# The last 512 features of an output projection computed with tokens as rows, and the last two recurrent heads' products spaced differently

## The chip, the cores and the metric

The kernel runs on one core of a Trainium2 chip. The metric is the device time of one execution in microseconds (us). The kernel before takes 1165.85 us, the median of three runs (1165.79 to 1166.35). A core has a matrix engine (TensorE, PE in the profile; PEld is its weight load), a vector engine (VectorE, DVE), an engine for activations and copies (ScalarE, ACT), a general one (GpSimd, POOL) and a queue engine for transfers (SyncE, SP). Each engine works through its own list of instructions in order and waits on semaphores for the others.

## The reference

One step of a two-layer decoder: layer 0 is a gated linear recurrence (HGRN2, 16 heads of 128), layer 1 is attention with a sliding window and sinks. Both end in an output projection and a LayerNorm over the residual. What matters here is that end, which layer 1 runs last of all, and the gated output of the recurrence:

```python
ALPHA = (2.0 * DEPTH) ** 0.25

# layer 0: o is the recurrence's output for 16 heads, g a projection of x
o = o * rsqrt(mean(o ** 2) + RMS_EPS) * norm_w            # per head
y = (o.reshape(bsz, t, 2048) * silu(g)) @ w_out           # 2048 x 2048

# layer 1: o is the attention's output
y = (o * silu(g)) @ w_out                                 # 2048 x 2048

# both
x = ALPHA * x + y
x = (x - mean(x)) * rsqrt(var(x) + LN_EPS) * ln_g + ln_b  # over 2048 features
```

There are 256 prompt tokens (and 16 meta tokens in layer 0, which are dropped after it) and 64 sample tokens, 8 sequences of 8. Everything is float32, and the LayerNorm of layer 1 gives the outputs `y_prompt` (256 x 2048) and `y_sample` (64 x 2048).

## The kernel before, in words

All activations lie with features as rows (partitions) and tokens as columns: `xh[k]`, `xl[k]` are feature block k (of 16) of the hidden state, split into a rounded high part and the remainder. A projection tile is 128 output features by all tokens. It is a sum over 16 feature blocks of three matmuls each, weight-low times x-high, weight-high times x-low, weight-high times x-high (lines 210 to 212). The weights (`lo`, `hi`) are what TensorE loads, 128x128, and the tokens are the moving columns: 336 in layer 0, 320 in layer 1's end.

The class `Stream` sets the order. It runs a list of chunks, each four feature blocks of one tile. After every feature block it calls `step()`, which advances up to two of the waiting "side" generators by one piece; a generator's `yield n` says after how many steps it wants its next turn. All work that isn't a projection (heads, epilogues, residuals) is interleaved with the projections in this way, and the written order is the order on each engine. The weights come ahead: `raw` (line 144) loads 512 KB pieces on SP's queue, 14 chunks ahead, into four buffers; `conv_hi` (L155, ACT) and `conv` (L166, DVE) make the two parts, some four to seven chunks ahead, in ten buffers.

**End of the recurrence.** Each head has a tail: `psp` and `pss` (state products, L657 and L661), `po` (its output, L689 to L701), the sum of squares and its power (`ss`, L706 to L708), `osc` (scaling, DVE L711), three transposes of osc (L717, into the bank `lv_b` of the next head, or `pt` for the last), and the gated output (L722) split into `oh`, `ol`. The projection tiles `z` of layer 0 read those. For the last head a fixed list of waits in steps says when head 14's and head 15's tails advance between the first z tiles. The first three z tiles, z0 to z2, are run chunk by chunk in turn. Their accumulators are three banks (`pj`) used before by the last tiles of the input projection, of which head 15's gate g is the last: DVE's L440 (`sg`, times g) is its reader.

**End of layer 1.** Sixteen tiles y0 to y15 of 128 features. For each, `residuals()` makes the LayerNormed hidden state `res` (POOL L1237, DVE L1239, POOL L1241, ACT L1243); `epi_y` adds it (DVE L1276, L1278), transposes the result to tokens as rows (L1286, three blocks: two of prompt tokens, one that holds the 64 sample tokens twice), takes the statistics (L1290) and multiplies by `ln_g` (L1302, L1306) into `z` and `zs`. After the last tile `stats()` (L1341 to L1368) finishes mean and power, makes a small matrix SL by a transpose, and `final_norm()` (L1371 to L1404) adds the mean and `ln_b` terms: nine matmuls R of SL with rows of g and b, then DVE (L1396) or ACT and POOL (L1392, L1393), and the twelve output transfers. `gb_parts()` prepares the rows of g and b beside the tiles, and `open_y()` loads g broadcast to all partitions on SP's queue.

## Time and profile before

| | |
|---|---|
| median of three runs | 1165.85 us |
| the profiled execution | 1166.44 us, its span 1164.2 us |
| mean granted clock of TensorE | 0.993 |
| TensorE busy | 1144.6 us, 98% of the span |
| VectorE busy | 789.5 us, 68% |
| ScalarE busy | 613.3 us, 53% |
| GpSimd busy | 237.9 us, 20% |
| transfers | 171.67 MB, 147 GB/s in the mean |
| z tiles of layer 0 | first product 570.3 us, last 701.0 us |
| y tiles of layer 1 | first product 1030.2 us, last 1147.6 us |

The span goes from the first to the last instruction of the profiled execution; some two microseconds lie around it. Overlapping matmuls are shown with their own length, so a matmul of "0.32 us" may start 0.15 us after the one before it. A row of the trace's timeline has the start, the duration, the engine, the line of the kernel, the operation, output and inputs, shapes, the count, and in brackets how long the engine had been idle and what released it.

### The profile page before, as it was taken

The page shows a single profiled execution, that of the slowest core. Times are in us where ns is not written, and L with a number is a line of the kernel's source. Part 1 is how long each engine was busy: PE and PEld are TensorE (multiplying, and loading weights), DVE is VectorE, ACT ScalarE, POOL GpSimd, SP SyncE. Part 2 cuts the span into 40 slices and gives each one's busy share as a digit, 9 for nine tenths or more (in the row PEclk, how much of TensorE's full clock was granted, in tenths as well). Part 3 has the DMA queues.
Part 4 walks back from the last instruction along what each step waited for, and adds up shares of the span by engine and source line. Part 5 has one row for each costly group of instructions (what it writes and reads, how often), then busy time and mean ns, then how long its engine had stood idle before and what let it go on. Part 6 is the DMA issues. An engine that isn't in the chain of part 4 may idle for free.

```text
span 1164.2 us, 26517 instructions
## 1 busy us (share of the span) xinstructions
PE 1144.6 (98%) x10225; PEld 1111.5 (95%) x10225; DVE 789.5 (68%) x2130; ACT 613.3 (53%) x1730; POOL 237.9 (20%) x344
## 2 busy tenths in 40 slices
PE   9999999999999999999899999999999999999995
PEld 8999999999999999999899999998999999999994
DVE  4766666666566666576668776577877767777674
ACT  5664555544555545554545444566666555554431
POOL 2131221211221212211224332100000112144311
PEclk9999999999999999999999999999999999999997
DMA  9644565454565455555445555643443535556532
GB/s 254 196 137 133 163 181 148 137 154 136 163 183 144 135 147 150 165 169 142 133 133 141 146 145 160 202 129 105 127 115 105 137 110 163 145 151 188 144 95 90
DMA packets 328908, 171.67 MB, mean 147 GB/s; under 512 B 19164, under 2 KB 325532, under 8 KB 328742
## 3 DMA queue, kind: packets, MB, share of 16 engines
q1 hardware_dynamic: 327184, 167.77, 51.6%
q8 instruction: 80, 1.31, 0.5%
q0 software_dynamic: 640, 1.18, 0.3%
q10 hardware_dynamic: 960, 1.05, 0.3%
q14 instruction: 44, 0.36, 0.1%
HBM read 157.17 MB, written 14.42 MB: 147 GB/s over the span
## 4 chain that ended last, share of the span: by engine, by line
PE 95%; DVE 1%; ACT 1%; DMA 1%; POOL 0%; issue 0%; SPq 0%; POOLq 0%; DVEq 0%
PE pj_g L210 7%; PE pj_g L211 7%; PE pj_g L212 7%; PE pj_q L210 7%; PE pj_q L211 6%; PE pj_q L212 6%; PE pj_f L210 3%; PE pj_z L212 3%; PE pj_z L211 3%; PE pj_z L210 3%; PE pj_i L210 3%; PE pj_f L211 3%; PE pj_i L212 3%; PE pj_i L211 3%; PE pj_f L212 3%; PE pj_y L210 3%
## 5 line engine op out<-in xcount | busy, mean ns | idle before, releaser
L210 PE MATMUL pj_q<-xh,wlo_q 128*128 128x336 f32 (+1 forms) x512 | 163.2, 319 | 0.0
L210 PE MATMUL pj_g<-xh,wlo_g 128*128 128x336 f32 (+1 forms) x512 | 163.0, 318 | 0.0
L211 PE MATMUL pj_g<-xl,whi_g 128*128 128x336 f32 (+1 forms) x512 | 160.7, 314 | 0.0
L211 PE MATMUL pj_q<-xl,whi_q 128*128 128x336 f32 (+1 forms) x512 | 160.6, 314 | 0.0
L212 PE MATMUL pj_g<-xh,whi_g 128*128 128x336 f32 (+1 forms) x512 | 160.5, 313 | 0.0
L212 PE MATMUL pj_q<-xh,whi_q 128*128 128x336 f32 (+1 forms) x512 | 160.3, 313 | 0.0
L210 PEld LDWEIGHTS pj_q<-xh,wlo_q 128*128 128x128 f32 x512 | 96.6, 189 | 2.5 <-issue 1.4
L210 PEld LDWEIGHTS pj_g<-xh,wlo_g 128*128 128x128 f32 x512 | 96.6, 189 | 0.7 <-issue 0.3
L211 PEld LDWEIGHTS pj_g<-xl,whi_g 128*128 128x128 f32 x512 | 96.8, 189 | 0.0
L211 PEld LDWEIGHTS pj_q<-xl,whi_q 128*128 128x128 f32 x512 | 96.7, 189 | 0.0
L212 PEld LDWEIGHTS pj_g<-xh,whi_g 128*128 128x128 f32 x512 | 96.6, 189 | 0.0
L212 PEld LDWEIGHTS pj_q<-xh,whi_q 128*128 128x128 f32 x512 | 96.6, 189 | 0.0
L166 DVE TENSOR_TENSOR wlo_g<-raw_g,whi_g 128x512 fp32r<-128x512 f32 x128 | 91.0, 745 | 0.2 <-ACT whi_g L155 0.2
L155 ACT CAST whi_g<-raw_g 128x512 fp32r<-128x512 f32 x128 | 76.5, 623 | 22.2 <-DMA raw_g<-in_hgrn_w_in_dram 17.7
L166 DVE TENSOR_TENSOR wlo_q<-raw_q,whi_q 128x512 fp32r<-128x512 f32 x128 | 85.1, 684 | 2.8 <-ACT whi_q L155 2.8
L619 POOL TENSOR_TENSOR vm<-Vs,cst 96x512 fp32r<-96x512 f32 x32 | 33.7, 1054 | 252.5 <-DVE Vs L616 251.5
L210 PE MATMUL pj_f<-xh,wlo_f 128*128 128x336 f32 x256 | 82.6, 323 | 0.0
L210 PE MATMUL pj_z<-oh,wlo_z 128*128 128x336 f32 x256 | 81.9, 320 | 0.0
L212 PE MATMUL pj_z<-oh,whi_z 128*128 128x336 f32 x256 | 81.6, 319 | 0.0
L210 PE MATMUL pj_i<-xh,wlo_i 128*128 128x336 f32 x256 | 81.5, 318 | 0.0
L211 PE MATMUL pj_z<-ol,whi_z 128*128 128x336 f32 x256 | 81.5, 318 | 0.0
L211 PE MATMUL pj_f<-xl,whi_f 128*128 128x336 f32 x256 | 81.1, 317 | 0.0
(398 smaller groups left out, 3229.1 us busy)
## 6 DMA issues: line engine op xcount, KB each, us to landing
raw_z<-in_hgrn_w_out_dram SPq DMA_DIRECT2D x32, 512.0 KB
raw_q<-in_swa_w_in_dram SPq DMA_DIRECT2D x32, 512.0 KB
raw_g<-in_swa_w_in_dram SPq DMA_DIRECT2D x32, 512.0 KB
raw_y<-in_swa_w_out_dram SPq DMA_DIRECT2D x32, 512.0 KB
raw_f<-in_hgrn_w_in_dram SPq DMA_DIRECT2D x30, 512.0 KB
raw_q<-in_hgrn_w_in_dram SPq DMA_DIRECT2D x30, 512.0 KB
raw_i<-in_hgrn_w_in_dram SPq DMA_DIRECT2D x30, 512.0 KB
raw_g<-in_hgrn_w_in_dram SPq DMA_DIRECT2D x30, 512.0 KB
```

The lines of the kernel that those rows point to most:

```text
L155: e.nc.scalar.copy(hi, t["raw", kc])
L166: e.nc.vector.tensor_tensor(lo, t.pop(("raw", kc)), hi.bitcast(F32), op=ALU.subtract)
L210: nc.tensor.matmul(ps, lo[:, kk, :], xh, start=first, stop=False)
L211: nc.tensor.matmul(ps, hi[:, kk, :], xl, start=False, stop=False)
L212: nc.tensor.matmul(ps, hi[:, kk, :], xh, start=False, stop=last)
L619: nc.gpsimd.tensor_tensor(vm[0:96, 4 * u:4 * u + 4, :], Vs[:, u, :].bitcast(F32).unsqueeze(1).to_broadcast([96, 4, P]), cst[0:96, 0:4].uns ...
```

## The change

**Rows instead of columns.** y0 to y11 stay. The last 512 features become one tile `yr` in which the tokens are what TensorE loads (128x128) and the weights are the moving 512 columns. It goes over three blocks of tokens: prompt tokens 0 to 127 and 128 to 255 with three products per feature block, and a third block of the sample tokens, once their high parts and once their low parts (copied to columns 320 to 384 of `ph`), which needs two products. The weights are loaded in runs of 512 columns, 2 feature blocks per transfer, converted per feature block, and all sixteen pairs are kept for blocks 1 and 2; six of the pairs lie in a new pool in the space of the hidden state, which is released before.

**Normalization by block.** The result has tokens as rows already. `normal` takes statistics, power and the LayerNorm of a prompt block and sends it while the next block's products run. `normal_sample` does the sample block after the last product. `stats`, `final_norm` and `gb_parts` go. g and b are loaded broadcast (3 MB in 16 transfers) on POOL's queue.

**Residuals.** Those of the last four feature blocks are made by a second generator beside the other tiles, transposed by 12 transposes `rt` in one go inside tile y6, and copied to `z`, `zs`. The other tiles' transposed results are copied by ACT, without the multiplication by g.

**Heads 14 and 15.** Another list of waits puts head 14's transposes behind more z products.

The core of the diff:

```diff
@@ run
+            if t.get("rows"):
+                while ("hl", kc) not in t:
+                    self.conv(self.nc + 1)
+                t["rows"](t, kc)
+                self.i += 1
+                continue
@@ head_chain, after the last head's products
-            yield 1
-            adv(h - 1)
-            yield 2
-            adv(h - 1)
-            yield 1
-            adv(h - 1)
-            yield 1
-            adv(h - 1)
-            yield 3
-            adv(h)
-            yield 1
-            adv(h)
-            yield 1
-            adv(h)
-            yield 3
-            adv(h)
-            for w in (4, 3, 2, 1):
+            for w, us in ((1, (h - 1,)), (3, (h - 1,)), (6, (h,)), (2, (h - 1, h)), (1, (h - 1, h)), (4, (h,)), (3, (h,)),
+                          (2, (h,)), (4, (h,)), (1, (h,))):
                 yield w
-                adv(h)
+                for u in us:
+                    adv(u)
@@ residuals
+                late = j >= LT
+                r = Y["p1"].tile([P, 384 if late else TY], F32, tag="resl" if late else "res", name=f"res{j}")
...
+                if late:
+                    nc.scalar.activation(r[:, 320:384], r[:, 256:320], AF.Identity, bias=lnb[0][:, j:j + 1])
+                nc.scalar.activation(rr, rr, AF.Identity, bias=lnb[0][:, j:j + 1])
@@ opening
+            for k in range(KT):
+                yield 4
+                nc.scalar.copy(L["oh1"][k][:, 320:384], L["ol1"][k][:, 256:320].bitcast(F32))
...
+            pts = [pm(f"rt{b}") for b in range(3)]
+            for b in range(3):
+                for i in range(4):
+                    nc.tensor.transpose(pts[b][:, 128 * i:128 * i + 128], Y["r", LT + i][:, 128 * b:128 * b + 128],
+                                        ident)
+            yield 1
+            for b in range(2):
+                nc.scalar.copy(Y["z"][:, b, 128 * LT:D], pts[b])
...
+            xps.close()
+            Y["cv"] = yes.enter_context(tc.tile_pool(name="wcx", bufs=6, side="right"))
+            yl = yes.enter_context(tc.tile_pool(name="ygb", bufs=1, side="right"))
+            for nm, src in (("g", ln_g), ("b", ln_b)):
+                t = Y[nm] = yl.tile([P, D], F32, tag=f"y{nm}", name=f"y{nm}")
+                for c in range(4):
+                    cs = slice(512 * c, 512 * c + 512)
+                    nc.gpsimd.dma_start(t[:, cs], src[1:2, cs].to_broadcast([P, 512]))
+                    yield 8
...
@@ epi_y
+                        nc.vector.bn_stats(Y["bn"][:, b, j, :], pt[:, 128 * b:128 * b + 128])
+                    nc.scalar.copy(Y["z"][:, :, 128 * j:128 * j + 128], pt[:, 0:256].rearrange("p (b f) -> p b f", b=2))
...
-                    nc.vector.tensor_tensor(Y["z"][:, :, cs], pt[:, 0:256].rearrange("p (b f) -> p b f", b=2),
-                                            Y["g"][:, cs].unsqueeze(1).to_broadcast([P, 2, P]), op=ALU.mult)
...
+        def block(t, k, b):
+            hi, lo = (x.rearrange("p k c -> p (k c)") for x in t["hl", k])
+            oh, ol = L["oh1"][k], L["ol1"][k]
+            cs = slice(128 * b, 128 * b + 128)
+            pairs = [(oh, lo), (oh, hi)] if b == 2 else [(oh, lo), (ol, hi), (oh, hi)]
+            for i, (x, w) in enumerate(pairs):
+                nc.tensor.matmul(t["ps", b], x[:, cs], w, start=k == 0 and i == 0,
+                                 stop=k == KT - 1 and i == len(pairs) - 1)
+                if i != 1:
+                    st.step()
+
+        def rows(t, k):
...
+            block(t, k, 0)
+            st.conv(st.i + e.DC)
+            if k < KT - 1:
+                return
+            while st.side:
+                st.step()
+            normal(t, 0)
+            for q in range(KT):
+                block(t, q, 1)
+            normal(t, 1)
+            for q in range(KT):
+                block(t, q, 2)
+            normal_sample(t)
...
+        def normal(t, b):
+            z = Y["z"][:, b, 128 * LT:D]
+            nc.vector.scalar_tensor_tensor(z, z, ALPHA, t["ps", b], op0=ALU.mult, op1=ALU.add)
+            nc.vector.bn_stats(Y["ag"][:, b, 3:9], z)
+            rs, nm = moments(b, 9)
...
+            for c, (z, g, bb) in enumerate(part):
+                if c == 0 or not b:
+                    centred(z, g, nm)
+                    if c == 0 and b:
+                        nr = Y["nr"]
+                        nc.vector.tensor_tensor(nr, nm, rs, op=ALU.mult)
+                        for zz, _, _ in part[1:]:
+                            nc.scalar.activation(zz, zz, AF.Identity, bias=nr, scale=rs)
+                    scaled(z, bb, rs)
+                else:
+                    nc.vector.tensor_tensor(z, z, g, op=ALU.mult)
+                    nc.vector.tensor_tensor(z, z, bb, op=ALU.add)
+                nc.sync.dma_start(y_prompt[0, 128 * b:128 * b + 128, 512 * c:512 * c + 512], z)
+
+        def normal_sample(t):
+            zs, S, ag = Y["zs"], t["ps", 2], Y["ag"]
+            for u in range(2):
+                us, fs = slice(64 * u, 64 * u + 64), slice(256 * u, 256 * u + 256)
+                z = zs[us, 768:1024]
+                nc.vector.scalar_tensor_tensor(z, z, ALPHA, S[0:64, fs], op0=ALU.mult, op1=ALU.add)
+                nc.vector.tensor_tensor(z, z, S[64:128, fs], op=ALU.add)
+            nc.vector.bn_stats(ag[:, 2, 3:9], zs[:, 768:1024])
+            nc.scalar.copy(ag[0:64, 2, 9:15], ag[64:128, 2, 3:9])
+            nc.vector.tensor_copy(ag[64:128, 2, 9:15], ag[0:64, 2, 3:9])
+            rs, nm = moments(2, 15)
...
+            for c in range(2):
+                cs = slice(512 * c, 512 * c + 512)
+                centred(zs[:, cs], Y["gs"][:, cs], nm)
+                scaled(zs[:, cs], Y["bs"][:, cs], rs)
...
```

`moments` is the aggregate (DVE), the power (POOL) and the negative mean (DVE); `centred` is (z - mean) x g and `scaled` is z x power + b, one DVE operation each.

What that makes of the engines' lists stands here at three places. A row is the line, the operation, output and inputs with the numbers of their buffers, the shape, and what it waits for. The first place is TensorE at the end of the recurrence, from head 15's transposes (`pv15`) to its `po15`; `pj_z0`, `pj_z1`, `pj_z2` are products of the first z tiles. Before:

```order
L589 MATMUL pv15_8411<-ident_110,iT_149 128x128 x3
L210 MATMUL pj_z0_8364<-oh2_628,wlo_z0_0_8144 128x336
...
L212 MATMUL pj_z1_8465<-oh2_628,whi_z1_0_8136 128x336
L717 MATMUL lv15_b_8371<-ident_110,osc14_8472 128x128 [waits DVE_49,Activation_49]
...
L210 MATMUL pj_z1_8465<-oh3_629,wlo_z1_0_8168 128x336
...
L210 MATMUL pj_z2_8495<-oh0_626,wlo_z2_0_8193 128x336
...
L657 MATMUL psp15_8507<-V15_8428,K15_8429 128x128 [waits PE_49,Activation_49]
...
L661 MATMUL pss15_0_8511<-vm15_8435,Ks15_8433 128x512 [waits PE_49,Pool_49]
...
L210 MATMUL pj_z2_8495<-oh3_629,wlo_z2_0_8193 128x336
...
L212 MATMUL pj_z0_8364<-oh7_633,whi_z0_1_8184 128x336
L689 MATMUL po15_8547<-S15_8518,qi1_161 32x128 [waits DVE_49,Activation_49]
```

Now:

```order
L606 MATMUL pv15_8411<-ident_110,iT_149 128x128 x3
L225 MATMUL pj_z0_8364<-oh2_628,wlo_z0_0_8144 128x336
...
L227 MATMUL pj_z1_8465<-oh3_629,whi_z1_0_8136 128x336
L225 MATMUL pj_z2_8484<-oh0_626,wlo_z2_0_8193 128x336 [waits DVE_49]
...
L227 MATMUL pj_z0_8364<-oh4_630,whi_z0_1_8184 128x336
L660 MATMUL psp15_8506<-V15_8428,K15_8429 128x128 [waits PE_49,Activation_49]
...
L664 MATMUL pss15_0_8510<-vm15_8435,Ks15_8433 128x512 [waits PE_49,Pool_49]
L664 MATMUL pss15_1_8512<-vm15_8435,Ks15_8433 128x512 [waits DVE_49,Activation_49]
L225 MATMUL pj_z0_8364<-oh5_631,wlo_z0_1_8285 128x336
...
L720 MATMUL lv15_b_8371<-ident_110,osc14_8477 128x128 x3
L225 MATMUL pj_z0_8364<-oh7_633,wlo_z0_1_8285 128x336
...
L692 MATMUL po15_8563<-S15_8525,qi1_161 32x128 [waits DVE_49,Activation_49]
```

There were 15 z products ahead of head 14's transposes and 12 between them and `psp15`. Now 33 stand between `pv15` and `psp15`, then the state products, 6 z products, the transposes, and 15 more z products ahead of `po15`. The first product of z2, before the fourth behind the transposes, is the 19th behind `pv15` and has a wait of its own on DVE.

The second place is DVE's list around the last weight pieces. Before, in tiles 13 and 14:

```order
L166 TENSOR_TENSOR wlo_y14_3_15625<-raw_y14_2_15435,whi_y14_3_15587 128x512 [waits Activation_49]
L166 TENSOR_TENSOR wlo_y15_0_15641<-raw_y15_0_15479,whi_y15_0_15612 128x512 [waits DMAHW2_49,Activation_49]
...
L1276 SCALAR_TENSOR_TENSOR z1_13_15674<-res13_15337,pj_y13_15589 128x256 [waits PE_49]
L1278 SCALAR_TENSOR_TENSOR z1_13_15674<-res13_15337,pj_y13_15589 128x128
L166 TENSOR_TENSOR wlo_y15_2_15677<-raw_y15_2_15526,whi_y15_2_15649 128x512 [waits DMAHW3_49,DVE_49,Activation_49]
L1290 BN_STATS ybn_14504<-yt13_15685 128x6 [waits PE_49]
...
L1302 TENSOR_TENSOR yz_14502<-yt13_15685,yg_14506 128x2x128
L1306 TENSOR_TENSOR yzs_14503<-yt13_15685,yg_14506 64x128
L166 TENSOR_TENSOR wlo_y15_3_15700<-raw_y15_2_15526,whi_y15_3_15665 128x512 [waits Activation_49]
L1276 SCALAR_TENSOR_TENSOR z1_14_15739<-res14_15426,pj_y14_15667 128x256 [waits PE_49]
```

Now, from tile 11's end into block 0 of the new tile `yr`:

```order
L170 TENSOR_TENSOR wlo_yr_5_15522<-raw_yr_4_15343,whi_yr_5_15494 128x512 [waits Activation_49]
L1318 SCALAR_TENSOR_TENSOR z1_11_15540<-res11_15218,pj_y11_15446 128x256 [waits PE_49]
L1320 SCALAR_TENSOR_TENSOR z1_11_15540<-res11_15218,pj_y11_15446 128x128
L170 TENSOR_TENSOR wlo_yr_6_15543<-raw_yr_6_15386,whi_yr_6_15514 128x512 [waits DMAHW2_49,DVE_49,Activation_49]
L170 TENSOR_TENSOR wlo_yr_7_15556<-raw_yr_6_15386,whi_yr_7_15530 128x512 [waits Activation_49]
L1331 BN_STATS ybn_14503<-yt11_15552 128x6 [waits PE_49]
...
L1341 BN_AGGR yag_14504<-ybn_14503 128x2 [waits DVE_49] x3
L1342 TENSOR_SCALAR yag_14504<-yag_14504 128x3 [waits DVE_49]
L170 TENSOR_TENSOR wlo_yr_8_15573<-raw_yr_8_15426,whi_yr_8_15547 128x512 [waits DMAHW3_49,Activation_49]
L170 TENSOR_TENSOR wlo_yr_9_15580<-raw_yr_8_15426,whi_yr_9_15558 128x512 [waits Activation_49]
...
L170 TENSOR_TENSOR wlo_yr_15_15622<-raw_yr_14_15545,whi_yr_15_15611 128x512 [waits Activation_49]
L1394 SCALAR_TENSOR_TENSOR yz_14510<-yz_14510,yr0_15532 128x512 [waits PE_49]
```

The pieces `wlo_yr_6` to `wlo_yr_15` stand behind tile 11's additions (`z1_11`), and the last eight of them behind its statistics and aggregations too; all of block 0's products need them in this order.

The third place is DVE's list at the end of the program. Before, from tile 15's last product:

```order
L1276 SCALAR_TENSOR_TENSOR z1_15_15798<-res15_15515,pj_y15_15732 128x256 [waits PE_49]
...
L1290 BN_STATS yag_14505<-yt15_15801 128x6 [waits PE_49]
...
L1344 BN_AGGR mv_15808<-yag_14505 128x2 [waits DVE_49,Pool_49]
...
L1351 TENSOR_SCALAR nm_15814<-mv_15808 128x3 [waits DVE_49]
...
L1358 TENSOR_TENSOR yS_14509<-mM_15815,rstd_15812 128x3x2 [waits DVE_49,Pool_49]
...
L1367 SCALAR_TENSOR_TENSOR yz_14502<-yz_14502,rstd_15812,yb_14511 128x512
L1302 TENSOR_TENSOR yz_14502<-yt15_15801,yg_14506 128x2x128
...
L1396 SCALAR_TENSOR_TENSOR yz_14502<-yz_14502,rstd_15812,R0_15835 128x512 [waits PE_49]
L1396 SCALAR_TENSOR_TENSOR yzs_14503<-yzs_14503,rstd_15812,R2_15839 128x512 [waits PE_49]
L1396 SCALAR_TENSOR_TENSOR yz_14502<-yz_14502,rstd_15812,R3_15841 128x512 [waits PE_49]
L1396 SCALAR_TENSOR_TENSOR yzs_14503<-yzs_14503,rstd_15812,R5_15845 128x512 [waits DVE_49,PE_49]
L1396 SCALAR_TENSOR_TENSOR yz_14502<-yz_14502,rstd_15812,R6_15847 128x512 [waits PE_49]
```

Now, from block 1's normalization (its middle part left out) to the end:

```order
L1394 SCALAR_TENSOR_TENSOR yz_14510<-yz_14510,yr1_15533 128x512 [waits PE_49]
L1395 BN_STATS yag_14504<-yz_14510 128x6 [waits DVE_49]
L1381 BN_AGGR ymv_14505<-yag_14504 128x2 [waits DVE_49]
...
L1405 TENSOR_TENSOR ynr_14508<-ynm_14506,yrs_14507 128x1 [waits Pool_49]
...
L1411 TENSOR_TENSOR yz_14510<-yz_14510,yb_15536 128x512 [waits DVE_49]
L1419 SCALAR_TENSOR_TENSOR yzs_14509<-yzs_14509,yr2_15534 64x256 [waits PE_49]
L1420 TENSOR_TENSOR yzs_14509<-yzs_14509,yr2_15534 64x256 [waits DVE_49]
...
L1421 BN_STATS yag_14504<-yzs_14509 128x6 [waits DVE_49]
L1423 COPY yag_14504<-yag_14504 64x6 [waits DVE_49]
L1381 BN_AGGR ymv_14505<-yag_14504 128x2 [waits DVE_49,Activation_49]
...
L1387 SCALAR_TENSOR_TENSOR yzs_14509<-yzs_14509,ynm_14506,ygs_15450 128x512 [waits DMASW5_49,DMASW3_49,DVE_49]
L1390 SCALAR_TENSOR_TENSOR yzs_14509<-yzs_14509,yrs_14507,ybs_15643 128x512 [waits DMASW3_49,DMASW5_49,DVE_49,Pool_49]
```

The part over all 384 rows that stood behind the last product (statistics, the matrix S, the corrections with R) is gone. What follows the last product (`yr2`) works on the sample rows: four additions of 64x256, statistics, aggregate and two times centred and scaled.

More of the change, by code (lines that the diff above doesn't have):

```diff
@@ L168, in conv, with add_rows @@
             self.nc += 1
+    def add_rows(self, t):
+        self.cseq += [(t, k) for k in range(KT)]
+        self.seq += [(t, k) for k in range(KT)]
     def step(self):
```

214 lines of the change are left out of this document (81 added, 133 removed).

## The prediction

> **What bounds the kernel now.** I read the page's totals first, then the chain that ended last, then TensorE's waits, and last the two places where the change works, instruction by instruction.
>
> ```profile
> span 1164.2 us, 26517 instructions
> PE 1144.6 (98%) x10225; PEld 1111.5 (95%) x10225; DVE 789.5 (68%) x2130; ACT 613.3 (53%) x1730; POOL 237.9 (20%) x344
> PE 95%; DVE 1%; ACT 1%; DMA 1%; POOL 0%; issue 0%; SPq 0%; POOLq 0%; DVEq 0%
> ```
>
> TensorE (PE) is busy for 98% of the span and holds 95% of the chain. So only three things can move the time: the number and length of matmuls, holes in TensorE's stream, and what comes after its last product. TensorE's waits (total, times, longest) name the holes:
>
> ```profile
> PE lv_b L717 <- DVE osc L711: 3.9, 1, 3.9
> PE pS L1363 <- DVE yS L1361: 2.6, 1, 2.6
> ...
> PE ln_rbc L845 <- DVE dg L841: 0.6, 1, 0.6
> ```
>
> The first is head 14's output transposes at the end of the recurrent layer. The second lies in the final normalization, after the last projection product. The change touches both; the third is outside it.
>
> **The junction at 574 to 588 us.** Columns: start, duration, engine, instruction, idle before it.
>
> ```profile
> 573.89 0.49 PE L589 MATMUL pv<-ident,iT 128*128 128x128 f32 x3
> 577.86 0.50 DVE L440 TENSOR_TENSOR sg<-sg,pj_g 128x336 f32<-128x336 f32 x1
> 579.93 0.56 DVE L711 TENSOR_TENSOR osc<-po,ss 128x384 f32<-128x384 f32 x1 [0.96 <-POOL ss L708]
> 580.64 0.88 PE L717 MATMUL lv_b<-ident,osc 128*128 128x128 f32 x3 [3.93 <-DVE osc L711]
> 587.86 0.30 PE L689 MATMUL po<-S,qi 128*32 128x128 f32 x1
> ...
> 563.17 0.94 PE L657 MATMUL psp<-V,K 128*128 128x128 f32 x6
> 564.40 0.49 PE L717 MATMUL lv_b<-ident,osc 128*128 128x128 f32 x3
> ...
> 299.94 0.32 PE L210 MATMUL pj_q<-xh,wlo_q 128*128 128x336 f32 x1
> 305.94 0.32 PE L210 MATMUL pj_q<-xh,wlo_q 128*128 128x336 f32 x1
> ```
>
> The last two rows stand 39 matmuls apart, 6.00 us, so a 336-column product takes 0.1538 us. psp with pss takes 564.40 - 563.17 = 1.23 us. Before, pv ends at 574.38, 15 projection products follow, and then TensorE stands for 3.93 us until head 14's osc is there (579.93 + 0.56). It pays a second time afterwards. Windows of the trace (PE and PEld busy, DVE, ACT, POOL, then the granted clock, DMA share, GB/s):
>
> ```profile
> 580.00:582.00 2.00, 1.36 (x6) 1.39 (x7) 1.53 (x4) 0.00 (x0) 0.80 (x1) 0.61 0.02 7
> 582.00:584.00 2.00, 2.00 (x10) 2.00 (x9) 1.46 (x7) 0.99 (x2) 1.09 (x1) 0.54 0.00 0
> 584.00:586.00 2.00, 2.00 (x16) 1.91 (x15) 0.77 (x3) 0.83 (x3) 0.00 (x0) 1.00 0.00 0
> ...
> 1142.30 0.33 PE yt L1286 x3
> ```
>
> The clock is at half for about 3.4 us. Three transposes take 0.33 us at full clock (last row, from the chain), so what runs from 580.64 to 587.86, 7.22 us, would be 27 x 0.1538 + 1.23 + 0.33 = 5.71 us: 1.51 us more are lost, 5.44 us in all.
>
> Now 33 products stand between pv and psp, then psp and pss, 6 products, the transposes, 15 products and po: 54 instead of 42 before po, twelve of them pulled in front of it. But the 19th of the 33 is the first of tile z2, which waits for DVE: its PSUM bank was pj_g's of head 15, and the sg row frees that only at 578.36. Eighteen products end at 574.38 + 18 x 0.1538 = 577.15, so a new stall of 1.25 us appears (with the 0.04 us between engines, to 578.40). DVE's sg stands behind the Ks and Vs subtractions, which the change does not move. From there 15 products reach 580.71, after osc (580.49), and nothing more waits: 580.71 + 1.23 + 6 x 0.1538 + 0.33 + 15 x 0.1538 = 585.50 for po. Before, po plus the twelve pulled products would be at 587.86 + 12 x 0.1538 = 589.71. **Term 1: -4.2 us.** Its bounds: -5.4 if the new stall does not exist, -2.6 if the stall also costs a clock window. What was hidden by head 14's early transposes is its gated output, which the projection needs only in its last quarter; nothing waits there.
>
> **The last 512 features: products.** For a 320-column product and for a 512-column one (pss, the only such product here):
>
> ```profile
> 1135.54 0.31 PE L210 MATMUL pj_y<-ph,wlo_y 128*128 128x320 f32 x1
> 1141.70 0.31 PE L210 MATMUL pj_y<-ph,wlo_y 128*128 128x320 f32 x1
> ...
> 563.86 0.70 PE L661 MATMUL pss<-vm,Ks 96*128 96x512 f32 x2
> ```
>
> 42 products in 6.16 us are 0.1467 us each. Four tiles of 48, each with three transposes, took 192 x 0.1467 + 4 x 0.33 = 29.49 us. From the end of psp shown above (564.11) to that of pss (564.56) two 512-column products take 0.45 us, 0.225 each; scaling 0.1538 by columns gives 0.2344; from pss's start to the next row's (564.40) it would be 0.27. I take 0.23, between the first two: ends and scaling describe a full stream, as this will be, while a start counts what is filled at its edge. The new 48 + 48 + 32 = 128 products take 29.44 us; tile 11's transposes (0.33) fall among them, and the residuals' 12 transposes, a new burst inside tile 6, cost 4 x 0.33 = 1.31. **Term 2: 29.44 + 0.33 + 1.31 - 29.49 = +1.6 us** (bounds +0.9 at 0.225 and +6.7 at 0.27). So there is no gain on TensorE: the sample block drops one product in three, but the tokens fill 384 rows instead of 320.
>
> **Can block 0 be fed?** These rows group the output stage (busy, mean ns of one):
>
> ```profile
> L166 DVE TENSOR_TENSOR wlo_y<-raw_y,whi_y 128x512 fp32r<-128x512 f32 x64 | 47.4, 772 | 0.2
> L1276 DVE SCALAR_TENSOR_TENSOR z<-res,pj_y 128x256 f32<-128x256 f32 x16 | 6.7, 419 | 23.0 <-PE pj_y L212 23.0
> L1296 DVE BATCH_NORM_AGGREGATE yag<-ybn 128x2 f32<-128x90 f32 x3 | 1.4, 515 | 0.0
> L1290 DVE BATCH_NORM_STATS2 yag<-yt 128x6 f32<-128x128 f32 x3 | 0.7, 288 | 0.4 <-PE yt L1286 0.4
> ...
> 596.38 2.49 DVE L166 TENSOR_TENSOR wlo_z<-raw_z,whi_z 128x512 fp32r<-128x512 f32 x4
> ```
>
> Block 0 eats sixteen weight pieces in 48 x 0.23 = 11.0 us, where the tiles before took a piece per 1.76 us. Six are converted when it starts. DVE owes it ten more at 2.49/4 = 0.62 us back to back, tile 11's two z rows (0.42 and about 0.28 for half the columns), three statistics (0.86) and three aggregations (1.55): 9.3 us, against the 10.35 us at which the last piece is needed. I cost this at nothing; at the mean row's 0.772 it would be 10.8, half a microsecond late (rival 2). Blocks 1 and 2 need no conversions.
>
> **The tail.** The chain after the last product, and the drain:
>
> ```profile
> 1147.76 0.16 PE pj_y L212
> 1150.01 0.90 POOL rstd L1346
> 1152.30 1.69 PE R L1385 x7
> 1157.14 1.22 POOL yz L1393
> ...
> 1158.39 0.34 ACTq L1404 DMA_DIRECT2D out_dram<-yz  x1
> 1161.00:1162.00 1.00, 0.00 (x0) 0.00 (x0) 0.00 (x0) 0.00 (x0) 0.00 (x0) 0.50 1.05 402
> 1162.00:1163.00 1.00, 0.00 (x0) 0.00 (x0) 0.00 (x0) 0.00 (x0) 0.00 (x0) 0.50 0.41 154
> ```
>
> From 1147.92 to 1164.2 are 16.28 us: statistics for 384 rows, the correction's matmuls, POOL's additions, and then twelve output transfers queued behind one another until about 1162.4 (a DMA share of 0.41 in the window from 1162). Now the normalization of blocks 0 and 1 and their transfers run beside blocks 1 and 2, and only 64 tokens remain. Rows for them:
>
> ```profile
> L1396 DVE SCALAR_TENSOR_TENSOR yz<-yz,rstd,R 128x512 f32<-128x512 f32 x4 | 2.9, 744 | 0.4 <-PE R L1385 0.4
> L1344 DVE BATCH_NORM_AGGREGATE mv<-yag 128x2 f32<-128x9 f32 x3 | 0.3, 160 | 0.0
> ```
>
> Block 1 on DVE while block 2 runs (32 x 0.23 = 7.4 us): z 0.74, statistics of 512 values about as much (between 0.288 and four times that), aggregate and nm 0.16 each, centred 0.74, nr 0.16, scaled 0.74, six multiplications and additions at about 0.68 (the conversions' size): 7.5 us, so the sample rows start 0.2 us late at most. They are: four 64x256 operations at 0.42 = 1.68; statistics of 256 values 0.42 (between 0.288 and its double); the exchange of the halves 0.3; aggregate 0.16; POOL's power 0.90, with nm and centred (0.90) beside it; scaled, centred, scaled 2.23; gaps 0.2: 5.9 us. Then four transfers of 128 KB. Old data ended 1.8 us before the span did; issue 0.34, a start of some 0.6 and 256 KB at 300 to 400 GB/s (0.7 to 0.85) make 3.5 us in all (bounds 2.8 without a start, 4.8 if the earlier block's transfers still queue). 0.3 + 5.9 + 3.5 = 9.7 us. **Term 3: 9.7 - 16.28 = -6.6 us** (bounds -7.5 and -5.1).
>
> The Trainium skill, "DMA: Bandwidth & Descriptors", in its fit for a transfer from GpSimd's queue, gives 2.0 us plus the bytes over 436 GB/s. By it the last 256 KB would take an estimated 2.6 us, and the sum would be 0.9 us lower; I stay with the rows of the drain.
>
> The old multiplications by g (32 on DVE) go; 48 small copies on ACT, half idle, replace them beside TensorE, and the late residuals go through POOL, 20% busy. I cost them at nothing: their cover is TensorE's 84 us of tiles 0 to 11, and without it a tile's chain could wait for POOL's residual, up to 1 us once.
>
> **Sum:** -4.2 + 1.6 - 6.6 = -9.2. The profiled execution took 1166.44 us (its span and 2.2 around it), 0.6 above the runs' median of 1165.85, so 1157.2 on its own time and 1156.7 on the median's. I say 1157.0.
>
> **Rivals.** *1. The clock falls after the new stall.* A hole of 1.25 us need not be free:
>
> ```profile
> 712.00:714.00 2.00, 2.00 (x15) 2.00 (x14) 1.52 (x4) 1.28 (x5) 1.78 (x5) 1.00 0.46 131
> 1150.00:1151.00 1.00, 0.00 (x0) 0.00 (x0) 0.97 (x4) 0.00 (x0) 0.89 (x1) 0.73 0.00 0
> ```
>
> For it: in the tail the clock fell in 1150 to 1151 though matmuls ran until 1147.92 and transposes after, so less than 3.4 us of a hole were enough there. Against: at 712 to 714, just behind the 0.6 us hole of ln_rbc, it stayed at 1.00. 1.25 lies between. Price: the 1.5 us measured at the junction, so 1158.5. The Trainium skill, "TensorE: Matmul & The Clock Gate", Part 1, says that the clock drops after at least one idle window of about 3.4 us. By that rule the hole costs no clock and 1157.0 stands; the trace agrees at 580 us and does not clearly in the tail.
>
> *2. Block 0 starves.* DVE at 0.772 per piece is 0.5 us late; the loads too must come at 512 KB per 1.38 us, 380 GB/s, near the 402 that the drain row shows, with four buffers. Late DVE also pushes block 1's normalization past block 2. About +2.5 us: 1159.5. Against: six pieces are ready and the rest of the loads were issued long before.
>
> *3. The other side: the broadcast of g and b holds off the weights.* It is 3 MB on POOL's queue, all issued in tiles 8 to 11 as soon as the space of the hidden state is free.
>
> ```profile
> masks<-in_consts_dram POOLq DMA_DIRECT2D x1, 528.0 KB, 6.7
> 1045.00:1050.00 5.00, 5.00 (x37) 4.99 (x36) 2.23 (x5) 1.18 (x3) 2.52 (x2) 1.00 1.05 329
> ```
>
> If POOL's queue gave what the masks' load shows (528 KB in 6.7 us, 79 GB/s) and the weights nothing meanwhile, the burst would last 40 us; the weights are loaded 14 pieces of 1.76 us ahead, 24 us, so TensorE would stand 16 us: 1173, slower. It decides from a blockade of about 24 + 9 = 33 us. Against it: at 1045 to 1050 the broadcast of g (there on SP) ran at 329 GB/s beside the weights, and TensorE was busy for 5.00 of 5.00 us; weights need 149 GB/s, so at 329 the 3 MB last 17 us beside them. The readers are late in any case: g is first wanted 11 us into the row blocks.
>
> **How the numbers follow.** Forecast 0.64, with its own range 1155.0 to 1159.0 (term 1 without the stall, term 3 at its bounds, term 2 at 0.2344). Rival 1 0.13, rival 2 0.15, rival 3 0.05. The remaining 0.03 is a product cost near 0.27, which gives 1162; with small stalls it is a no-change case. Measurement of this kernel tells 0.2%, 2.3 us, so faster means below 1163.5. Faster 0.91, same 0.04, slower 0.05. The range 1153.9 to 1161.5 takes the forecast and the first two rivals in, up to 2 us of rival 2 beyond its price.
>
> **What would show it.** At the junction: TensorE's wait for osc gone from the list of waits, a wait of 1.2 us of z2's first product for sg in its place, po's start near 585.5, granted clock 1.00 throughout (a window below 1 is rival 1). In the row blocks: products 0.23 us apart, 11 us per prompt block, no wait for wlo (rival 2 would show as one in block 0). In the tail: about 6 us of DVE rows of 64x256 and 128x512 after the last product, 9.7 us to the end, and the clock there without effect since TensorE has nothing left. A TensorE wait for wlo or raw pieces in tiles 8 to 11 is rival 3. The prediction is wrong at its root if TensorE needs 0.27 us per product, or if the wait at the junction only moves to another head's rows.

## The result, and the profile after

The changed kernel takes 1158.84 us (median of four runs, 1157.71 to 1159.38), beside 1166.1 us for the kernel before on the same chip. The ratio is 0.9926 with a 95% interval of 0.9906 to 0.9946. On another occasion the same kernel, run five times more, had a median of 1158.09 us beside 1166.46 (ratio 0.9927, 0.9914 to 0.9939). Forecast were 1157.0 and a range of 1153.9 to 1161.5.

The profiled execution took 1157.71 us with a span of 1155.7; that of before took 1166.44 with 1164.2. The head of its page, and the engines' shares of the chain that ended last:

```profile
span 1155.7 us, 26360 instructions
PE 1141.5 (99%) x10151; PEld 1104.2 (96%) x10151; DVE 795.2 (69%) x2094; ACT 620.2 (54%) x1771; POOL 238.9 (21%) x343
PE 95%; DVE 2%; DMA 1%; ACT 1%; issue 0%; SPq 0%; POOL 0%; DVEq 0%
```

The first rows of TensorE's waits (us in total, times, longest):

```profile
PE pj_z L225 <- DVE sg L457: 1.3, 1, 1.3
PE pw L319 <- DVE mhalf L274: 1.1, 1, 1.1
```

Both large waits of before (3.9 us for osc, 2.6 us for the matrix S) are gone. One of 1.3 us is new: tile z2's first product waits for the last head's gate. The second, at the start of the program, was there before. Here is the junction in the timeline of the change (start, duration, engine, instruction, idle before it and its releaser):

```profile
573.61 0.49 PE L606 MATMUL pv<-ident,iT 128*128 128x128 f32 x3
577.59 0.50 DVE L457 TENSOR_TENSOR sg<-sg,pj_g 128x336 f32<-128x336 f32 x1
578.15 0.42 PE L225 MATMUL pj_z<-oh,wlo_z 128*128 128x336 f32 x1 [1.26 <-DVE sg L457]
585.37 0.30 PE L692 MATMUL po<-S,qi 128*32 128x128 f32 x1
```

And the windows of the change behind it; the third number from the right is the granted clock:

```profile
578.00:580.00 2.00, 1.85 (x12) 1.85 (x13) 0.93 (x3) 1.94 (x6) 1.90 (x2) 1.00 0.86 258
580.00:582.00 2.00, 2.00 (x15) 1.91 (x14) 1.96 (x3) 0.27 (x1) 0.95 (x2) 1.00 0.02 6
```

The hole is 1.26 us, where 1.25 were forecast, and the clock stays at 1.00. From pv to po it takes 585.37 - 573.61 = 11.76 us; the forecast had 585.50 - 573.89 = 11.61. Before, the same way took 13.97 us with twelve products fewer, 15.82 with them: the junction gained 4.06 us.

The end of the program, from the chain of the change that ended last (start, duration, engine, line):

```profile
1115.50 1.38 PE yr L1356 x6
1116.89 0.45 PE yt L1328 x3
1117.34 20.69 PE yr L1356 x90
...
1145.01 0.69 DVE yz L1411
1145.70 0.33 DVE yzs L1419
1147.40 0.44 DVE yag L1421
1150.89 0.75 DVE yzs L1390
```

And its last windows, with DMA share and GB/s at the right:

```profile
1153.00:1154.00 1.00, 0.00 (x0) 0.00 (x0) 0.00 (x0) 0.00 (x0) 0.00 (x0) 0.50 0.91 251
1154.00:1155.00 1.00, 0.00 (x0) 0.00 (x0) 0.00 (x0) 0.00 (x0) 0.00 (x0) 0.50 0.00 1
```

96 products of 512 columns take 22.07 us, 0.230 each, and follow one another without a hole in this execution except for 0.12 us at `yt` (0.45 in place of 0.33). The last 32 bring the last product's end to about 1138.03 + 32 x 0.23 = 1145.39. VectorE is then 0.3 us late with block 1's last part (its end is at 1145.70), works on the sample rows until 1151.64, and the data are out by about 1154; the span ends at 1155.7. So the tail is 10.3 us, of which 4.1 lie behind the last operation: 2.4 until the data are out and 1.7 behind them. Before, the data moved longer than the prediction's windows of one microsecond let it seem. In half a microsecond of the kernel before, less than 1.7 us ahead of the span's end (1164.2):

```profile
1162.50:1163.00 0.50, 0.00 (x0) 0.00 (x0) 0.00 (x0) 0.00 (x0) 0.00 (x0) 0.50 0.15 57
```

### The profile page after: what moved, and what is told of

It is laid out like the page before. It is cut to its first block, busy times and chain, and to the rows that moved or that the text cites. A ratio compares the mean times of both kernels' runs of the same rounds, so it can differ in the third digit from the quotient of the medians.

```text
span 1155.7 us, 26360 instructions
## 1 busy us (share of the span) xinstructions
PE 1141.5 (99%) x10151; PEld 1104.2 (96%) x10151; DVE 795.2 (69%) x2094; ACT 620.2 (54%) x1771; POOL 238.9 (21%) x343
## 3 DMA queue, kind: packets, MB, share of 16 engines
q8 instruction: 80, 1.31, 0.5%
## 4 chain that ended last, share of the span: by engine, by line
PE 95%; DVE 2%; DMA 1%; ACT 1%; issue 0%; SPq 0%; POOL 0%; DVEq 0%
PE pj_g L225 7%; PE pj_g L226 7%; PE pj_g L227 7%; PE pj_q L225 7%; PE pj_q L226 6%; PE pj_q L227 6%; PE pj_f L225 3%; PE pj_i L225 3%; PE pj_z L225 3%; PE pj_f L226 3%; PE pj_i L227 3%; PE pj_z L227 3%; PE pj_i L226 3%; PE pj_f L227 3%; PE pj_z L226 3%; PE pj_y L225 2%
```

## The experiments

All times are medians; each group names the kernel before that ran beside it. TensorE's wait for the very first input varies between executions (0.4 to 1.3 us in the traces here), so places of two traces are compared by distances, not by their clock times.

### The two parts apart

The change without the new spacing, and the spacing alone on the kernel before:

```diff
# rows_only: the change, with the old list for the last head
-            for w, us in ((1, (h - 1,)), (3, (h - 1,)), (6, (h,)), ...):
-                yield w
-                for u in us:
-                    adv(u)
+            yield 1
+            adv(h - 1)
...
# spacing_only: the kernel before, with the new list
-            yield 1
-            adv(h - 1)
...
+            for w, us in ((1, (h - 1,)), (3, (h - 1,)), (6, (h,)), ...):
```

> The change without the new spacing of heads 14 and 15 (their old list of waits). Theory: the parts add up, and the spacing is worth 4.2 us, so this kernel is 4.2 us slower than the change, about 1163.0 us or 3.1 us below the kernel before; TensorE waits 3.9 us for head 14's osc again, with the clock near half behind it. Rival: the gain is all in the row blocks and the tail, and the stall at the junction is made good later by something else that would have waited; then it equals the change, 1158.8.

> The kernel before with only the new list of waits of heads 14 and 15. Theory: 4.2 us faster than the kernel before, about 1161.9, with a stall of 1.26 us of tile z2's first product on the gate's multiplication in place of the 3.9 us. Rival: the freed time is lost again before layer 0 ends (another wait appears in the z tiles): within 1 us of before.

Beside 1166.57 us before, the rows alone took 1163.24 (1161.67 to 1164.49; ratio 0.9975, 0.9965 to 0.9984) and the spacing alone 1161.62 (ratio 0.9961, 0.9949 to 0.9974). So the parts are worth 3.3 and 4.9 us, and their sum, 8.3, is what the change gives (7.3 and 8.4 in its two measurements). The traces show the two patterns in TensorE's waits, first with the rows alone, then with the spacing alone:

```profile
PE lv_b L734 <- DVE osc L728: 3.9, 1, 3.9
```

```profile
PE pS L1349 <- DVE yS L1347: 2.6, 1, 2.6
PE pj_z L210 <- DVE sg L440: 1.3, 1, 1.3
```

The spacing gave what was expected. In its trace po comes 11.75 us behind pv (573.31 to 585.06), 4.07 better than before with the twelve products counted in; pv itself stands 0.6 us earlier than before's, so part of the 4.9 is the start. The rows gave less: terms 2 and 3 were -5.0 together. The profiled execution of the rows alone, 1161.67, does lie 4.8 below the profiled one of before, but it is the shortest of its eleven, and they spread over 2.8 us. That spread is taken up below.

### The new stall

Taken away, by issuing the last head's gate multiplication ahead of the splitting of K and V and pulling one more feature block of products ahead of the state products:

```diff
                 def chain():
-                    yield 2
+                    yield 2 if h < H - 1 else 1
                     nc.vector.tensor_tensor(sg, sg, ps, op=ALU.mult)
...
-            for w, us in (..., (6, (h,)), ...
+            for w, us in (..., (7, (h,)), ...
```

> The change, with the last head's gate multiplication one step earlier, so that it stands ahead of the splitting of K and V on VectorE, and one more feature block of z products ahead of the state products. Theory: the 1.26 us stall goes and nothing waits in its place (0.2 us at most, for osc): 1.2 us faster than the change, about 1157.6, a mean granted clock unchanged. Rival 1 of the prediction (the clock falls behind that stall in those executions that were 1 us longer than the profiled one): 2.3 us faster at the median, about 1156.5, and a smaller spread between executions.

It took 1157.41 us (ratio 0.9925, 0.9912 to 0.9937, beside 1166.57), 1.4 below the change's first median and 0.7 below its second. The junction shows it without the noise of the start:

```profile
574.00 0.49 PE L606 MATMUL pv<-ident,iT 128*128 128x128 f32 x3
585.08 0.30 PE L692 MATMUL po<-S,qi 128*32 128x128 f32 x1
```

Here po comes 11.08 us after pv, with three products more ahead of it (0.46 us): 1.14 us better than the change's 11.76, as expected. The spread stayed at 2.3 us (1156.48 to 1158.80), so the stall and the clock behind it are not, or not alone, what makes the executions differ.

Made longer, by one, two or three extra multiplications of 0.50 us ahead of the gate's on VectorE, whose results nobody reads:

```diff
                     yield 2
+                    if h == H - 1:
+                        scr = hp1.tile([P, T], F32, tag="scr", name="scr")
+                        for _ in range(3):    # 1 in gap_1, 2 in gap_2
+                            nc.vector.tensor_tensor(scr, sg, ps, op=ALU.mult)
                     nc.vector.tensor_tensor(sg, sg, ps, op=ALU.mult)
```

> The change, with three multiplications of 128x336 (0.50 us each, into a scratch tile that nobody reads) ahead of the last head's gate multiplication on VectorE, so that TensorE's stall at the junction grows from 1.26 to 2.76 us. Theory: a hole that is shorter than one window leaves the clock at 1.00, and the time grows by the hole alone, 1.5 us, to 1160.3. Rival: a window with mostly idle time in it is enough, as the tail of the kernel before suggested: the clock falls to about 0.55 for one window of 3.4 us and 1.5 us more are lost, 1161.8.

> As the kernel with three extra multiplications ahead of the gate, but with one: a stall of about 1.8 us at the junction instead of 1.26 (change) or 2.86 (three). If the clock falls only for holes near 2.9 us, the clock stays at 1.00 and the time is 0.5 us above the change, about 1158.9. If the limit lies below 1.8 us, a window near 0.5 shows behind the stall and po starts 1.3 us later still, 1160.2.

> The same with two extra multiplications: a stall of about 2.35 us. Without a fall of the clock 1.1 us above the change, about 1159.5; with it 1160.8 and a window near 0.5 behind the stall.

Medians: one 1159.44, two 1160.01 (beside 1166.7), three 1161.35 (beside 1166.57). TensorE's wait in the timeline and the windows behind it, for one, two (with pv and po) and three, each in a fence:

```profile
578.86 0.42 PE L225 MATMUL pj_z<-oh,wlo_z 128*128 128x336 f32 x1 [1.79 <-DVE sg L461]
580.00:582.00 2.00, 2.00 (x17) 2.00 (x16) 1.76 (x3) 0.15 (x1) 0.76 (x2) 1.00 0.08 22
```

```profile
574.33 0.49 PE L610 MATMUL pv<-ident,iT 128*128 128x128 f32 x3
579.94 0.42 PE L225 MATMUL pj_z<-oh,wlo_z 128*128 128x336 f32 x1 [2.34 <-DVE sg L461]
580.00:582.00 2.00, 2.00 (x9) 2.00 (x10) 1.26 (x3) 0.69 (x2) 1.25 (x2) 0.62 0.24 72
582.00:584.00 2.00, 2.00 (x10) 2.00 (x9) 2.00 (x2) 0.00 (x0) 2.00 (x1) 0.52 0.05 12
588.68 0.30 PE L696 MATMUL po<-S,qi 128*32 128x128 f32 x1
```

```profile
579.76 0.65 PE L225 MATMUL pj_z<-oh,wlo_z 128*128 128x336 f32 x1 [2.86 <-DVE sg L461]
580.00:582.00 2.00, 2.00 (x8) 2.00 (x9) 1.26 (x3) 0.00 (x0) 2.00 (x2) 0.50 0.01 3
```

Holes of 1.26 and 1.79 us left the clock alone; holes of 2.34 and 2.86 us brought it to half for one window. With the hole of 2.34 us po comes 14.35 us after pv, 2.59 more than in the change: 1.08 for the longer hole and 1.51 for the clock, the price that rival 1 had. The Trainium skill, "TensorE: Matmul & The Clock Gate", Part 1, asks for at least one idle window of about 3.4 us; the trace doesn't agree, since 2.34 us were enough. These are single executions. With two extra multiplications the four times reach from 1159.07 to 1161.05 us, and the one with the trace is the longest, so the clock need not have fallen in all of them. Each of the three medians lies between the two forecasts made for it. So where exactly the limit lies, and whether it moves from one execution to the next, stays open.

### The broadcast of g and b, and the spread

```diff
-                    nc.gpsimd.dma_start(t[:, cs], src[1:2, cs].to_broadcast([P, 512]))
+                    nc.sync.dma_start(t[:, cs], src[1:2, cs].to_broadcast([P, 512]))
# and so the four transfers of the sample rows' g and b
```

> The change itself once more, beside the three others on the same chip. Theory: 7.3 to 8.5 us below the kernel before, 1158 to 1159. Its trace of another execution should again show the junction's stall of 1.26 us with the clock at 1.00, 0.23 us per product in the row blocks without a hole, and about 10.3 us from the last product to the end; what makes other executions some 1 us longer than the profiled one (spans 1156.7 to 1157.3 against 1155.7) should stand in it. If it is the clock behind the stall, one window below 1 is in it; if it is the start, TensorE's wait for the first inputs is longer; if it is the row blocks, a wait for weights is there.

> The change with the 16 broadcast transfers of g and b (3 MB) on SP's queue in place of POOL's. Theory: they are hidden either way, since TensorE never waits for weights in tiles 8 to 11; same time within 0.5 us. Rival 3 in a mild form (the burst on POOL's queue disturbs the weights in some executions): up to 1.5 us faster at the median, with a smaller spread. A third way: in SP's own order the burst stands ahead of weight pieces and holds them up, which would show as a wait for weights and a slower time.

Beside 1166.46 us before, the change took 1158.09 (1157.69 to 1158.95) and the kernel with the transfers on SP's queue 1157.63 (1157.28 to 1157.81; ratio 0.9922, 0.9908 to 0.9935). The medians differ by 0.5 us, within what the theory allowed, but the spread fell from 1.3 to 0.5 us, as the rival had it. The change's second trace was again one of a short execution, with 0.2 us lost at tile 11's transposes. What a longer one can hold showed in a trace of another kernel that has the change's row blocks, the one with another split of the last rows (below). Its longest wait of TensorE, and then the chain that ended last in that kernel:

```profile
PE yt L1328 <- DVE z L1318: 1.2, 1, 1.2
```

```profile
1097.84 16.27 DMA raw_yr<-in_swa_w_out_dram
...
1115.51 0.63 ACT whi_yr L159
...
1116.16 0.07 DVE wlo_yr L170
...
1116.77 0.42 DVE z L1318
...
1117.23 0.55 PE yt L1328 x3
```

One weight piece of the row blocks takes 16 us from issue to landing. Its conversion on ACT, then on VectorE, comes late, and tile 11's sum z stands behind it in VectorE's list. So TensorE, six products into block 0, waits 1.2 us at tile 11's transposes. In the change's profiled execution the same z was late by only 0.12 us.

The late piece itself is in the short executions too. Here are ACT's wait for it in the change's second trace, the conversion of the sixth piece and tile 11's z; then the same conversion and z with SP's queue:

```profile
1113.71 0.62 ACT L159 CAST whi_yr<-raw_yr 128x512 fp32r<-128x512 f32 x1 [4.67 <-DMA raw_yr<-in_swa_w_out_dram]
1115.68 0.69 DVE L170 TENSOR_TENSOR wlo_yr<-raw_yr,whi_yr 128x512 fp32r<-128x512 f32 x1 [0.62 <-ACT whi_yr L159]
1116.29 0.41 DVE L1318 SCALAR_TENSOR_TENSOR z<-res,pj_y 128x256 f32<-128x256 f32 x1
```

```profile
1112.23 0.69 DVE L170 TENSOR_TENSOR wlo_yr<-raw_yr,whi_yr 128x512 fp32r<-128x512 f32 x1 [0.17 <-ACT whi_yr L159]
1115.46 0.42 DVE L1318 SCALAR_TENSOR_TENSOR z<-res,pj_y 128x256 f32<-128x256 f32 x1 [2.54 <-PE pj_y L227]
```

With SP's queue the sixth piece is converted 3.4 us earlier, and z waits for TensorE's products alone. With POOL's queue z stands behind a late conversion, and what that costs TensorE was nothing to 0.2 us in the other traces and 1.2 us in the one above.

The windows of the stage before, first of the change, with its transfers of g behind them (count, size, us from issue to landing), then of the kernel with SP's queue (second number from the right: DMA share; last: GB/s):

```profile
1096.00:1100.00 4.00, 4.00 (x29) 4.00 (x28) 2.55 (x6) 2.92 (x6) 1.21 (x3) 1.00 1.05 305
1108.00:1112.00 4.00, 4.00 (x30) 3.99 (x30) 2.58 (x7) 1.14 (x2) 0.00 (x0) 1.00 1.05 244
yg<-in_ln_g_dram POOLq DMA_DIRECT2D x4, 256.0 KB, 8.0
```

```profile
1096.00:1100.00 4.00, 4.00 (x29) 4.00 (x29) 2.47 (x6) 2.92 (x6) 0.00 (x0) 1.00 0.32 114
1108.00:1112.00 4.00, 4.00 (x30) 3.99 (x29) 3.04 (x8) 1.06 (x3) 0.00 (x0) 1.00 0.65 198
```

On POOL's queue nothing holds the burst back, and it shares the DMA engines with the weights while they are fully busy. On SP's queue the transfers stand one by one among the weight pieces, which wait for their buffers, so the burst is stretched: b's last transfers go out at 1119 to 1121 us, when the last weights are under way. This is rival 3's mechanism, at less than a tenth of its price. A range like that of the eleven executions of the rows alone, 2.8 us, is more than the 1.2 us seen, and none of the long ones has a trace. Two other causes are not ruled out. The mean granted clock of those eleven goes from 0.993 to 0.996, and four of the five longest have 0.994, while the change's nine lie at 0.996 to 0.998. And TensorE's first wait alone differs by 0.9 us between traces. So the rest is open.

### Where the tail's gain is from

```diff
# blocks_mixed: blocks 1 and 2 alternate
             for q in range(KT):
                 block(t, q, 1)
-            normal(t, 1)
-            for q in range(KT):
                 block(t, q, 2)
+            normal(t, 1)
             normal_sample(t)
```

> The change with the products of the second prompt block and of the sample block alternating, feature block by feature block, so that both end together and the second prompt block's normalization has no products beside it. Theory: its 7.6 us on VectorE then stand behind the last product, ahead of the sample rows: 7.3 us slower than the change, about 1165.5, within 1 us of the kernel before; the time from the last product to the end grows from 10.3 to about 17.7 us. Rival: the old tail was long because of its transfers and POOL's additions, which are gone either way; then less than 3 us slower, about 1161.

It took 1164.75 us (ratio 0.9984, 0.9975 to 0.9994, beside 1166.85). The chain shows all the products of blocks 1 and 2 in one piece, and the last operation:

```profile
1117.49 27.55 PE yr L1356 x120
1157.89 0.75 DVE yzs L1389
```

The last product ends at 1145.04 and the span at 1162.7, 17.7 us later, as expected, where the change has 10.3. So the tail's gain is the overlap of block 1's normalization with block 2's products. With the tokens as rows but no overlap there, the tail is 1.4 us longer than the 16.28 us of before: all of its gain is lost. The 2.1 us that are left of the median are no more than the junction's 4.1 can supply.

A first attempt to show this moved both calls of the normalization behind the last product in the text:

```diff
-            normal(t, 0)
             for q in range(KT):
                 block(t, q, 1)
-            normal(t, 1)
             for q in range(KT):
                 block(t, q, 2)
+            normal(t, 0)
+            normal(t, 1)
             normal_sample(t)
```

> The change with the normalization of both prompt blocks moved behind the last product of the sample block, so that nothing of it runs beside products. Theory: the tail's gain is the overlap, not the layout; 7.8 us for block 0 and 7.5 us for block 1 on VectorE then stand in the tail ahead of the sample rows, so it is about 15 us slower than the change, 1174, and slower than the kernel before. Rival: the old tail was long because of its transfers and POOL's additions, which are gone in either case; then 5 us slower at most, 1164.

It took 1158.63 us, the time of the change. Moving the calls in the text behind TensorE's products moved nothing on VectorE: each engine's list came out the same as in the change, and VectorE still starts as soon as its block is done. The experiment tested nothing. It served as another sample of the change, and its trace has the same late weight piece (15.3 us) and a wait of 0.2 us at tile 11's transposes.

### The last transfers

The kernel with the early gate, and the sample rows' last normalization in 768 and 256 columns:

```diff
-            for c in range(2):
-                cs = slice(512 * c, 512 * c + 512)
+            for c, (c0, n) in enumerate(((0, 768), (768, 256))):
+                cs = slice(c0, c0 + n)
```

> The kernel with the early gate multiplication, and the sample rows' last normalization split into 768 and 256 columns in place of 512 and 512, so that the last two transfers carry 64 KB each in place of 128. Theory: 1.2 us from the junction as before, and 0.5 us from the tail (0.1 on VectorE, 0.4 us less data behind the last operation): 1.7 us below the change, about 1157.0 where the change has 1158.7. Rival: the end of the last transfer is a fixed time after its issue, whatever its size, and the first two transfers start 0.5 us later: no more than the junction's 1.2 us.

It took 1157.31 us (ratio 0.9921, 0.9907 to 0.9934, beside 1166.46), no more than the junction's gain. From the last product to the end it took 10.4 us, as in the change. The last operation ends 6.3 us behind the last product in both. The first two transfers go out 0.5 us later than in the change and carry more, the last two carry half; the end comes 4.1 us behind the last operation as before. The last two are issued 6.3 us behind the last product in both kernels and end at the same distance with half the bytes. Whether the later and larger first ones hold them up, or their time doesn't depend on their size, this run doesn't separate.

### Both findings in one kernel

The early gate of `gate_early` and the SP queue of `bcast_sp`:

> Both findings in one kernel: the last head's gate multiplication ahead of the splitting of K and V with one more feature block of z products, and the broadcast transfers of g and b on SP's queue. Theory: 1.1 us less than the kernel with the transfers moved (1157.6), about 1156.5, and executions within 1 us of one another, since the weights of the row blocks no longer come late; TensorE waits neither for the gate nor for tile 11's sums. Rival: the late weights aren't the cause of the spread, and executions still reach from 1156 to 1159.

It took 1156.35 us (1156.19 to 1156.74; ratio 0.9910, 0.9896 to 0.9925, beside 1166.85), and its four executions lie within 0.6 us. Tile 11's transposes are back to their plain length in the chain:

```profile
1114.44 1.39 PE yr L1356 x6
1115.82 0.33 PE yt L1328 x3
1116.15 20.69 PE yr L1356 x90
```

It is faster than the change by 1.7 us (against its second median) to 2.5 (against its first), and its spread is that of the kernel with SP's queue, where the change and the early gate alone spread over 1.3 to 2.3 us. So the spread was small both times that the transfers stood on SP's queue, with four executions each. That the late weights are what spreads the others is likely but not shown, since no long execution of the change has a trace.

## Why the prediction was right, point by point

- **Term 1, the junction (-4.2).** Right in its steps and its size. The trace has the new stall at 1.26 us on the gate, po 11.76 us behind pv (11.61 forecast), no fall of the clock, and no new wait behind it; alone it measured 4.9 us with an interval of 3.0 to 5.9 (0.9974 and 0.9949 of 1166.57).
- **Term 2, the products (+1.6).** Right: 0.230 us per product, 22.07 us for the first 96. From block 0's start to the last product are 29.9 us, against 29.44 + 0.33 forecast. The residuals' 12 transposes stand from 1075.01 to the next product at 1076.24 us, 1.23 us, against 1.31.
- **Term 3, the tail (-6.6).** Right in mechanism, mis-sized by 0.6: 10.3 us in place of 9.7. VectorE's part was right (6.3 us from the last product to the last operation, 6.2 forecast). The drain was not: 4.1 us from the last operation's end to the span's end, where 3.5 stood. From the last operation to the last data it took 2.4 us, where issue, start and bytes were put at 1.7. The 1.8 us behind the last data was misread in the trace of before, where data still moved after 1162.5, but it came near the change's 1.7. The estimate of 2.6 us by the Trainium skill, "DMA: Bandwidth & Descriptors", is for a transfer alone, and the prediction set it against the whole drain. Set against the 2.4 us it was the better figure, though it was worked out for another queue.
- **"Six are converted when it starts"; block 0 costed at nothing.** This step failed. At block 0's start (1115.50 us) VectorE had not yet begun the sixth piece, since the weights landed late under the burst on POOL's queue. The cost was 0.12 us in the profiled execution and 1.2 us in another trace, and it did not come through missing weights for a product, as rival 2 had it, but through tile 11's sum, which stands behind the conversion in VectorE's list. The row of 329 GB/s that was held against rival 3 was right for the total rate; it said nothing of which queue's transfers wait. With the transfers on SP's queue the sixth piece's conversion began 3.2 us ahead of block 0 (1112.23 and 1115.42), so the assumption held there.
- **Rival 1** didn't happen at 1.26 us, and its price of 1.5 us was right when the hole was made 2.34 us long. **Rival 3** happened in a mild form: 1.2 us in one trace, where 9 would have been needed to turn the sign.
- **The number.** The profiled execution, at 1157.71, lies 0.5 us above the 1157.2 forecast on its own time: the drain's 0.6, the junction's 0.15 and tile 11's 0.12, less a start that was 0.3 us earlier (pv at 573.61 in place of 573.89), which is luck. The medians, 1158.84 and 1158.09, lie 1.1 to 1.8 us above 1157.0. What the executions behind them hold beyond the profiled ones, 0.4 to 1.1 us, stands in no trace of the change. Late weights are the likeliest cause, since moving the transfers took 0.5 us off the median and narrowed the spread, but the start and the clock are not ruled out.

## What to carry to other kernels

When a stall is filled with other work, look up who holds the buffer of the first filled-in item; here it was a one-line gate multiplication behind the splitting of K and V, and moving it one step gave another 1.1 us. A load that is wanted late should not be issued without anything to hold it back: here, on a queue of its own, it took the DMA engines from those wanted early, and in the queue of the others it waited its turn. And on an engine that works through its list in order, a late input is paid by whatever stands behind its reader, not by the reader alone.

## What the runs showed of the hardware

The granted clock fell to half for about 3.4 us at holes of 2.34 and 2.86 us in TensorE's stream and didn't at 1.26 (six traces) and 1.79. All but the hole of 1.26 us stand on one execution each. The end of the span lies about 1.7 us behind the last data, and 4.1 us behind the last operation, whether the last two transfers carry 128 KB each or 64. A 512 KB weight load took up to 16.3 us from issue to landing while 3 MB of broadcast loads were under way on another queue.
